# Low part of the keys kept twice, so that both products of the attention scores read 128 rows; indexer heads two at a time

## The chip, the cores and the metric

The program runs on one core of a Trainium2 chip. The metric is device time in microseconds (us), the median of three runs. The engines are named as in the profile: PE is TensorE's matrix multiply and PEld its weight loads, DVE is VectorE, ACT is ScalarE, POOL is GpSimd, and SP is SyncE, whose queue issues the DMAs.

## What is computed

A decoder trunk of four residual blocks on 1024 tokens of width 1024, in float32. Layer 0 is attention of two kinds (eight "forgetting" heads with a data-dependent bias, four differential heads with two softmax maps each), then a gated feed-forward block. Layer 1 is sparse attention of eight heads, whose keys an indexer picks, beside eight stick-breaking heads, then a second feed-forward block. The part that matters here, cut from the reference:

```
# every attention: scores of 64-wide heads, for 128 queries at a time
s = jnp.einsum('bqhd,bkhd->bhqk', qb, k).astype(jnp.float32) * scale
...
# the indexer of the sparse heads: four heads of 64, one key for all of them
logits = jnp.einsum('bqhd,bkd->bqhk', iqb, ik).astype(jnp.float32)
score = jnp.einsum('bqhk,bqh->bqk', jax.nn.relu(logits), iwb.astype(jnp.float32))
score = jnp.where(kpos[None, None, :] <= qpos[None, :, None], score, -jnp.inf)
_, sel = lax.top_k(score, top_k)          # top_k = 256
```

## The kernel before

Each float32 operand of a product is held as a rounded high part and a low part, the rest. A general product is three matmuls (`three`): high by high, high by low, low by high. The scores do it with two. A query block of a head stands as a stack of 128 rows, 64 of the high part and 64 of the low part (`evac_q`; of the two heads of a pair one has the high part on top, the other the low part). The high part of the keys, `kh`, is kept twice, in both halves of the rows (`evac_k`: ACT copies the PSUM result to one tile, and three DMAs between tiles of SBUF move halves so that each of two tiles has its head's rows twice). So one matmul of 128 rows gives high by high and low by high at once. The low part of the keys, `kl`, has the rows of both heads in one tile, each once. The second matmul takes the 64 rows of the query's high part and the 64 rows of this head's low keys:

```python
self.mm(s[:, c:c + w], q, KH[c // 512][:, :w], True, False)
self.mm(s[:, c:c + w], q[r], KL[c // 512][r, :w], False, last)
```

Keys come in chunks of at most 512 columns (c). Query block i (128 queries, i from 0 to 7) has 128 (i + 1) keys, so blocks 0 to 3 have one chunk and blocks 4 to 7 two: 12 chunks a head, and as many pairs of a `kh` and a `kl` matmul. A third, bfloat16 matmul adds the causal mask at the last block where there is one (`cmask`, `smask`). The scores lie in `psS`, which has two buffers of 1024 columns.

Layer 0 makes 16 such sets of scores (eight heads, and four with two maps each), layer 1 eight stick-breaking heads (`stick`) and eight sparse ones (`dsa`). With the indexer's 40 pairs (four heads, query blocks 2 to 7) there are 32 x 12 + 40 = 424 pairs.

The engines' order is static. `heads` runs the heads one after the other: for each, the rows of scores and softmax of query blocks 0 to 7 (`sm`) are woven with the transposes and value products of the head before (`av`), and with pieces of a generator (`fill`) that projects the queries, keys and values of later heads. A scheduler with a model of the engines' times then sets the order on each engine; an engine takes its instructions in that order. The SP queue too is taken in order: an instruction on it that waits holds back all that stand behind it.

In layer 1 the indexer (`index`) comes first: per half of the tokens four projections (`proj_tok`), transposes, `evac_q` of both pairs of heads into four tiles `iq`, then for each query block the four heads' scores, a Relu on ACT to `rl` and an accumulation on DVE to `sc`. The 256 best of each row are found by bisection on the bits of the scores (`topk`, 32 rounds): for three of six query blocks DVE counts what is over the bound (L988, written to scratch `jv`), for the others ACT does (L990, scratch `junk`). A round is issued behind a scan of the stick-breaking heads (L754), and the sparse heads need the result.

Of the kernel before, what the change touches and what calls it, by code (L numbers as in the profile page):

```python
# [13 lines left out]
I32 = mybir.dt.int32  # L14
U32 = mybir.dt.uint32
# [26 lines left out]
class Halves:  # L42
    """what is made of each half of the tokens, made when first asked for"""
# [10 lines left out]
class Net:  # L54
# [13 lines left out]
    # ---------------------------------------------------------------- tools  # L68
# [22 lines left out]
    def new_x(self):  # L91
        """eight token tiles of x"""
        X = [self.vp.tile([P, 4, D], F32, name="x", tag="v", bufs=2) for _ in range(2)]
        return [X[t // 4][:, t % 4] for t in range(NT)]

    def new_v(self):
        """values of four heads of 64 (or two of 128)"""
        return self.vp.tile([P, NT, 2, 2, P], F32R, name="v", tag="v", bufs=2)

    def identity(self):  # L100
# [3 lines left out]
        self.junk = cst.tile([P, D], mybir.dt.int8, name="junk")  # L104
# [97 lines left out]
    def mean_square(self, src, n):  # L202
        """1/sqrt(mean(src^2) + eps), a column"""
# [8 lines left out]
    def norm_half(self, xt, g):  # L212
        """four token tiles, normed and transposed and split: hT hi and lo"""
# [17 lines left out]
    def three(self, out, sh, sl, mh, ml, start, stop):  # L231
        """out += s.T @ m with both operands split; s stationary"""
# [4 lines left out]
    def proj_T(self, w, h):  # L237
        """[128 columns, 512 tokens]; a generator that returns them"""
# [7 lines left out]
    def proj_tok(self, units, h, t, n):  # L246
        """[128 tokens, n columns]; units: (hi, lo) pieces over d"""
# [10 lines left out]
    # ------------------------------------------------------- q, k, v stacks  # L258
# [24 lines left out]
    def scores(self, i, Q, KH, KL, r, mask):  # L283
        """psum scores of query block i; the operands are pairs of halves"""
# [3 lines left out]
        for c in range(0, n, 512):  # L288
# [3 lines left out]
            self.mm(s[:, c:c + w], q[r], KL[c // 512][r, :w], False, last)  # L292
# [4 lines left out]
    def pair(self, qs, ks):  # L297
        """two heads' operands of the scores"""
        (QA, QB), (KA, KB, KL) = zip(*qs), zip(*ks)
        return (QA, KA, KL, slice(0, 64)), (QB, KB, KL, slice(64, 128))  # L300

    def projected(self, us, h, gate):
        """a pair of heads; a generator"""
# [13 lines left out]
    def av(self, pt, H, half):  # L317
        """transposes the P blocks of a half of the queries, and sums over keys; a generator"""
# [51 lines left out]
    def chain(self, jobs):  # L370
        """jobs: (gate, load, body): the weights of a job are loaded before the body of the one before"""
# [28 lines left out]
    def after(self, n, f):  # L400
        """f is traced n pieces from now"""
        self.later.append([n, f])
# [8 lines left out]
    def weave(self, A, B, nb, rate):  # L411
        """the pieces of A and the generator B (of nb pieces) in step, with rate pieces of fill"""
# [40 lines left out]
    def evac_head(self, pool, feat):  # L453
        """stores the products of v hi and of v lo, [64, 512] each, of the head's output"""
# [10 lines left out]
    def softmax_rows(self, pool, i, s, bias, tag=""):  # L465
        """p = exp(s + bias - max); returns p and its sum"""
# [3 lines left out]
        m = pool.tile([P, 1], F32, name="mx", tag="mx", bufs=6)  # L470
        l = pool.tile([P, 1], F32, name="sm", tag="sm", bufs=6)
# [9 lines left out]
    def rope(self, v, M, t, pool):  # L481
        """v: [128 tokens, M, >=16]; the first 16 of each are turned, in place"""
# [3 lines left out]
        tm = pool.tile([P, 4, M, 8], F32, name="rp", tag=f"rp{M}", bufs=2)  # L486
# [8 lines left out]
    def v_split(self, ps, V, t, n):  # L495
        """psum [128 tokens, heads x n] to hi n | lo n of each head"""
# [5 lines left out]
    # ------------------------------------------------------------- layer 0  # L502
    def even_attn(self, h):
        nc, tc, A = self.nc, self.tc, self.A
        with ExitStack() as st:
# [62 lines left out]
            def fox(hd):  # L568
# [5 lines left out]
                def sm(i):  # L574
# [5 lines left out]
                    r = pp.tile([P, 1], F32, name="rc", tag="rc", bufs=6)  # L580
# [39 lines left out]
            def diff(hd):  # L620
# [3 lines left out]
                def sm(i):  # L624
# [3 lines left out]
                    m2 = pp.tile([P, 1], F32, name="mx", tag="mx", bufs=6)  # L628
                    l2 = pp.tile([P, 1], F32, name="sm", tag="sm", bufs=6)
# [5 lines left out]
                    r1 = pp.tile([P, 1], F32, name="rc", tag="rc", bufs=6)  # L635
                    r2 = pp.tile([P, 1], F32, name="rd", tag="rd", bufs=6)
# [44 lines left out]
            def zipped(f, g):  # L681
                """the pieces of f, and with each a piece of g"""
# [29 lines left out]
    # ------------------------------------------------------------- layer 1  # L712
    def odd_attn(self, h):
        nc, tc, A = self.nc, self.tc, self.A
        unit = partial(self.wunit, lo_eng="vector")
        with ExitStack() as st:
# [53 lines left out]
            def dsa_q(g, us):  # L770
                """rotated queries of four heads, to memory"""
# [10 lines left out]
            def dsa_load():  # L782
                """what the sparse attention needs, into the room of h"""
# [54 lines left out]
            def dsa(hd):  # L838
# [6 lines left out]
                def sm(i):  # L845
# [6 lines left out]
                    r = pp.tile([P, 1], F32, name="rc", tag="rc", bufs=6)  # L852
# [47 lines left out]
    def index(self, h, ix, iw, sc, chd, cld, krd):  # L900
        """latent keys, rope key (both to memory), and the scores of the indexer; a generator"""
        nc, A = self.nc, self.A
        IK = [self.qk.tile([P, 512], F32R, name="kh", tag="kh", bufs=6) for _ in range(2)]
        IL = [self.qk.tile([P, 512], F32R, name="kl", tag="kl", bufs=4) for _ in range(2)]
# [36 lines left out]
        for half in range(2):  # L941
            IQ = [ix.tile([P, 512], F32R, name=f"iq{a}", tag=f"iq{a}", bufs=1) for a in range(4)]
# [8 lines left out]
            for a in range(2):  # L951
                self.evac_q(tr(xs, a * P, (a + 1) * P), IQ[2 * a], IQ[2 * a + 1])
            yield
            for i in range(max(2, 4 * half), 4 * half + 4):
# [3 lines left out]
                for a in range(4):  # L958
                    r = slice(0, 64) if a % 2 == 0 else slice(64, 128)
                    s = self.scores(i, (IQ[a],) * 2, IK, IL, r, None)  # L960
                    rl = self.Y("rl")
                    nc.scalar.activation(rl[:, :n], s, AF.Relu)
                    nc.vector.scalar_tensor_tensor(sc[i], rl[:, :n], iw[:, i, a:a + 1], sc[i],
                                                   op0=ALU.mult, op1=ALU.add)
                    yield
# [418 lines left out]
```

## Time and profile before

| | |
|---|---|
| median of three runs | 2906.18 us |
| lowest and highest run | 2903.67 and 2909.28 us |
| span of the profiled execution, first to last instruction | 2899.5 us |
| time of the profiled execution itself | not listed apart from its span; the median of the runs is 6.7 us above the span |
| PE busy | 2776.9 us, 96% of the span |
| DVE, ACT, POOL busy | 1780.4, 1324.4, 790.2 us |
| mean granted TensorE clock | 0.975 of full speed |

Read it so: the span is what the trace covers, and the 6.7 us between it and the median is taken as what lies around it. Matmuls are pipelined and the ends of their records are modelled, so the busy time of PE holds overlaps and stalls; what one matmul costs is seen from its start to the start of the next. Attention of layer 0 takes some 60 to 590 us, its feed-forward block is done by some 1430 us, the indexer's scores lie between 1500 and 1580 us, stick-breaking and the bisection between 1585 and 1930 us, the sparse heads go to 2100 us, and the rest is the second feed-forward block.

### The profile page before, as it was taken

What the parts mean: (1) busy time and instruction counts of PE and PEld (TensorE: products, weight loads), DVE (VectorE), ACT (ScalarE), POOL (GpSimd) and SP (SyncE); (2) the same over time, 40 slices, a digit from 0 to 9 for tenths busy, and PEclk for the clock granted to TensorE, in tenths of its full rate; (3) what the DMA queues carried; (4) which work ended last, traced back from release to release, by engine and by line L of the source; (5) the groups of instructions that cost most, each with busy time, mean ns of one, the idle gap of its engine ahead of it and who ended that gap; (6) DMA issues with size and microseconds to landing.
All of it is one profiled execution on the core that took longest, in us unless ns stands there. A gap on an engine that the chain in (4) does not pass through costs nothing.

```text
span 2899.5 us, 38031 instructions
## 1 busy us (share of the span) xinstructions
PE 2776.9 (96%) x14352; PEld 2237.3 (77%) x14352; DVE 1780.4 (61%) x2561; ACT 1324.4 (46%) x2218; POOL 790.2 (27%) x1039
## 2 busy tenths in 40 slices
PE   7999999989899999999999999889998999999998
PEld 6778788779688888787887777546697888887886
DVE  3554554544777777443434998987646777776344
ACT  4444543432444444333334777646624444443232
POOL 0333433440433333000130333343504333330000
PEclk9999999989999999999999999779999999999999
DMA  5331221332232223441211222313531322223421
GB/s 113 107 88 42 74 50 38 102 116 88 69 98 75 78 87 120 142 152 44 88 52 48 66 72 87 87 39 73 172 109 66 101 82 73 87 84 139 166 77 58
DMA packets 118952, 254.47 MB, mean 88 GB/s; under 512 B 36136, under 2 KB 39336, under 8 KB 118640
## 3 DMA queue, kind: packets, MB, share of 16 engines
q1 hardware_dynamic: 118768, 252.04, 28.2%
q8 instruction: 113, 1.85, 0.3%
q14 instruction: 71, 0.58, 0.1%
HBM read 168.33 MB, written 56.92 MB: 78 GB/s over the span
## 4 chain that ended last, share of the span: by engine, by line
PE 84%; DVE 8%; ACT 2%; issue 2%; DMA 2%; POOL 1%; SPq 1%; POOLq 0%; DVEq 0%; ACTq 0%
PE psB L82 38%; PE psS L82 31%; PE psO L82 11%; PE psB L345 3%; DVE t L754 2%; DVE jv L988 1%; DVE ptl L188 1%; PE psB L1127 1%; DMA ro<-ot 0%; SPq L131 0%; PE psB L225 0%; PE psB L897 0%; DVE xn L1116 0%; DVE T_vector L1002 0%; DVE la L188 0%
## 5 line engine op out<-in xcount | busy, mean ns | idle before, releaser
L188 DVE TENSOR_TENSOR ptl<-psB,pth 128x512 fp32r<-128x512 f32 x280 | 182.2, 658 | 108.3 <-ACT pth L351 99.7
L82 PE MATMUL psB<-ha,hh 128*128 128x256 f32 (+1 forms) x768 | 222.8, 291 | 6.2 <-DVE kl L188 3.1
L82 PE MATMUL psB<-la,hh 128*128 128x256 f32 (+1 forms) x768 | 218.5, 285 | 0.0
L82 PE MATMUL psB<-ha,hl 128*128 128x256 f32 (+1 forms) x768 | 218.1, 285 | 0.0
L351 ACT ACTIVATE pth<-psB 128x512 fp32r<-128x512 f32 x280 | 158.4, 574 | 126.8 <-PE psB L345 86.7
L188 DVE TENSOR_TENSOR al<-ar,ah 128x512 fp32r<-128x512 f32 x88 | 61.0, 693 | 251.0 <-ACT ah L1228 248.2
L209 POOL TENSOR_TENSOR rs<-rs,mhalf 128x1 f32<-128x1 f32 x48 | 33.1, 693 | 627.6 <-DVE rs L208 627.3
L188 DVE TENSOR_TENSOR la<-ra,ha 128x1024 fp32r<-128x1024 f32 (+1 forms) x92 | 116.9, 1271 | 139.8 <-ACT ha L1134 112.0
L1228 ACT ACTIVATE ah<-ar 128x512 fp32r<-128x512 f32 x88 | 55.5, 631 | 311.2 <-PE psO L82 298.1
L345 PE MATMUL psB<-identf,p 128*128 128x128 f32 x1008 | 172.9, 283 | 13.5 <-DVE p L640 6.6
L82 PE MATMUL psS<-kh,qs 128*128 128x512 f32 (+2 forms) x384 | 166.9, 435 | 18.6 <-ACT p L474 5.6
L82 PE MATMUL psS<-kl,qs 64*128 64x512 f32 (+2 forms) x384 | 178.9, 466 | 0.0
L82 PE MATMUL psO<-pth,v 128*128 128x512 f32 (+2 forms) x384 | 151.5, 402 | 6.6 <-ACT pth L351 4.1
L82 PEld LDWEIGHTS psB<-ha,hh 128*128 128x128 f32 x768 | 147.2, 192 | 9.7 <-DVE kl L188 3.6
L345 PEld LDWEIGHTS psB<-identf,p 128*128 128x128 f32 x1008 | 127.5, 145 | 34.5 <-DVE p L640 7.2
L82 PEld LDWEIGHTS psB<-la,hh 128*128 128x128 f32 x768 | 146.8, 191 | 1.3 <-issue 0.4
L1134 ACT ACTIVATE ha<-ra 128x1024 fp32r<-128x1024 f32 x44 | 46.6, 1060 | 220.3 <-DMA ra<-in_wi_dram 182.1
L82 PEld LDWEIGHTS psB<-ha,hl 128*128 128x128 f32 x768 | 146.4, 191 | 0.8 <-issue 0.6
L1134 ACT ACTIVATE hs<-sr 128x1024 fp32r<-128x1024 f32 x88 | 92.8, 1055 | 115.4 <-PE psB L82 99.7
L1169 POOL TENSOR_TENSOR sr<-rb 128x512 f32<-128x512 f32 x44 | 59.1, 1343 | 314.8 <-issue 289.6
L82 PE MATMUL psO<-ptl,v 128*128 128x512 f32 x336 | 134.1, 405 | 11.2 <-DVE ptl L188 11.0
L82 PE MATMUL psS<-la,ah 128*128 128x512 f32 x352 | 138.4, 393 | 0.4 <-DVE la L188 0.4
(360 smaller groups left out, 8365.3 us busy)
## 6 DMA issues: line engine op xcount, KB each, us to landing
ra<-in_wi_dram SPq DMA_DIRECT2D x44, 512.0 KB, 4.1
rb<-in_wi_dram SPq DMA_DIRECT2D x44, 512.0 KB, 3.6
act<-yc SPq DMA_DIRECT2D x44, 512.0 KB, 3.3
ar<-act SPq DMA_DIRECT2D x88, 256.0 KB, 2.8
wd<-in_wd_dram SPq DMA_DIRECT2D x28, 512.0 KB, 4.5
kh<-kh SPq DMA_DIRECT2D x96, 128.0 KB, 2.3
ot<-oa SPq DMA_DIRECT2D x96, 128.0 KB, 2.4
ro<-ot SPq DMA_DIRECT2D x24, 512.0 KB, 3.6
```

The costliest lines, as they stand in the source:

```text
L82: self.nc.tensor.matmul(out, lhsT, rhs, start=start, stop=stop, skip_group_check=True)
L188: getattr(self.nc, eng).tensor_tensor(dst, src, hi.bitcast(F32), op=ALU.subtract)
L209: nc.gpsimd.tensor_tensor(rs, rs, self.mhalf[:, 0:1], op=ALU.pow)
L345: nc.tensor.transpose(t[:, c:c + P], H.pr[q][:, j * P:(j + 1) * P], self.identf)
L351: nc.scalar.activation(hi[:, :used], t[:, :used], AF.Copy)
L754: scan = nc.vector.tensor_tensor_scan(t1[:, :n][:, ::-1], s[:, ::-1], self.zeros[:, 0:1].to_broadcast([P, n]), 1.0, ALU.mult, ALU.add)
L988: nc.vector.tensor_scalar(j[:, :n], x, t, 0.0, op0=op, op1=ALU.add, accum_out=out)
L1127: nc.tensor.transpose(t_[:, t * P:(t + 1) * P], xs[t][:, d * P:(d + 1) * P], self.identf)
L1134: self.nc.scalar.activation(hi, raw, AF.Copy)
L1169: nc.gpsimd.tensor_tensor(s12[:, 0:4], rv[:, 0:4], rv[:, 4:8], op=ALU.add)
L1228: nc.scalar.activation(ah, ar, AF.Copy)
```

## The change

`evac_k` now makes two tiles of low keys as it does of high ones, each with its head's 64 rows twice: `new_k` takes two `kl` tiles a head pair and half (six buffers in place of four), and three DMAs `kl<-kl` of 64 x 512 join the three `kh<-kh` (32 calls, 96 DMAs more). `scores` multiplies the whole stack of the query with the doubled low keys, so the product of the two low parts, left out before, is added. The indexer's `IL` already had its rows twice. In `index` the zeroing of `sc` moves ahead, and the heads go two at a time: two tiles `iq` in place of four, each with one buffer, so the second pair's `evac_q` can write only after the last score of the first pair. Scratch: `jv` and `te` are int8 in place of bfloat16, `rp` has one buffer in place of two, `mx`, `sm`, `rc`, `rd` four in place of six. The remaining lines of the diff are comments.

```diff
     def new_k(self):
-        return [self.qk.tile([P, 512], F32R, name=n, tag=n, bufs=b) for n, b in (("kh", 6), ("kh", 6), ("kl", 4))]
+        return [self.qk.tile([P, 512], F32R, name=n, tag=n, bufs=b) for n, b in (("kh", 6), ("kh", 6), ("kl", 6), ("kl", 6))]
...
-    def evac_k(self, ps, KA, KB, KL):
+    def evac_k(self, ps, KA, KB, LA, LB):
         self.nc.scalar.activation(KA, ps, AF.Copy)
-        self.lo("vector", KL, ps, KA)
-        for dst, src in ((KB[64:128], KA[64:128]), (KB[0:64], KA[64:128]), (KA[64:128], KA[0:64])):
-            self.nc.sync.dma_start(dst.bitcast(F32), src.bitcast(F32))
-        return KA, KB, KL
+        self.lo("vector", LA, ps, KA)
+        for A, B in ((KA, KB), (LA, LB)):
+            for dst, src in ((B[64:128], A[64:128]), (B[0:64], A[64:128]), (A[64:128], A[0:64])):
+                self.nc.sync.dma_start(dst.bitcast(F32), src.bitcast(F32))
+        return KA, KB, LA, LB
...
-            self.mm(s[:, c:c + w], q[r], KL[c // 512][r, :w], False, last)
+            self.mm(s[:, c:c + w], q, KL[c // 512][:, :w], False, last)
...
-        tm = pool.tile([P, 4, M, 8], F32, name="rp", tag=f"rp{M}", bufs=2)
+        tm = pool.tile([P, 4, M, 8], F32, name="rp", tag=f"rp{M}", bufs=1)
...
-            for a in range(2):
-                self.evac_q(tr(xs, a * P, (a + 1) * P), IQ[2 * a], IQ[2 * a + 1])
-            yield
             for i in range(max(2, 4 * half), 4 * half + 4):
                 n = P * (i + 1)
                 nc.gpsimd.memset(sc[i][:, :n - P], 0.0)
                 nc.gpsimd.tensor_scalar(sc[i][:, n - P:], self.cmask, 1.0, 1.0, op0=ALU.mult, op1=ALU.mult)
-                for a in range(4):
-                    r = slice(0, 64) if a % 2 == 0 else slice(64, 128)
-                    s = self.scores(i, (IQ[a],) * 2, IK, IL, r, None)
...
+            for b in range(2):
+                IQ = [ix.tile([P, 512], F32R, name=f"iq{a}", tag=f"iq{a}", bufs=1) for a in range(2)]
+                self.evac_q(tr(xs, b * P, (b + 1) * P), *IQ)
+                yield
+                for i in range(max(2, 4 * half), 4 * half + 4):
+                    n = P * (i + 1)
+                    for a in range(2):
+                        s = self.scores(i, (IQ[a],) * 2, IK, IL, None)
...
-                j = jpool.tile([P, S], BF16, name="jv", tag="jv", bufs=1)
+                j = jpool.tile([P, S], I8, name="jv", tag="jv", bufs=1)
...
```

Where instructions move. On the SP queue, at the first pair of heads of layer 0 (`ra` are weights, `qs` and `ql` the query stacks, `nb` and `ndr` the bias rows), the rows stand so before:

```order
L272 DMA qs<-qs 64x512
L272 DMA qs<-ql 64x512 x2
L280 DMA kh<-kh 64x512 x3
L272 DMA qs<-qs 64x512
L195 DMA ra<-in_w0t_dram 128x1024
L272 DMA qs<-ql 64x512 x2
L533 DMA ndr<-nrow 8x1024
```

and so in the changed kernel:

```order
L273 DMA qs<-qs 64x512
L273 DMA qs<-ql 64x512 x2
L282 DMA kh<-kh 64x512 x2
L282 DMA kl<-kl 64x512 x2
L282 DMA kh<-kh 64x512
L282 DMA kl<-kl 64x512
L273 DMA qs<-qs 64x512
L196 DMA ra<-in_w0t_dram 128x1024
L273 DMA qs<-ql 64x512 x2
L536 DMA ndr<-nrow 8x1024
```

Three copies of low keys stand between the copies of high keys and all that follows, here the next query stack, a piece of weights and the bias rows.

On PE, at a query block 4 of layer 0 whose second chunk of keys is newly made (`identf,p` are transposes for the value product), the order before is:

```order
L82 MATMUL psS<-kh,qs 128x512
L82 MATMUL psS<-kl,qs 128x512
L82 MATMUL psS<-kh,qs 128x256
L82 MATMUL psS<-kl,qs 128x256
L82 LDWEIGHTS identb
L82 MATMUL psS<-cmask,identb 128x128
L345 MATMUL psB<-identf,p_2121 128x128 x3
L82 MATMUL psS<-kh,qs 128x512
```

and in the changed kernel:

```order
L83 MATMUL psS<-kh,qs 128x512
L83 MATMUL psS<-kl,qs 128x512
L83 MATMUL psS<-kh,qs 128x256
L348 MATMUL psB<-identf,p_2145 128x128 x3
L83 MATMUL psS<-kh,qs 128x512
L83 MATMUL psS<-kl,qs 128x512
L83 MATMUL psS<-kh,qs 128x256
L83 MATMUL psS<-kl,qs 128x256
L83 LDWEIGHTS identb
L83 MATMUL psS<-cmask,identb 128x128
L83 MATMUL psS<-kl,qs 128x256
L83 LDWEIGHTS identb
```

The second product with the new low keys has moved behind the transposes and behind the scores of the next block. The same happens at a handful of other places; elsewhere the order of PE in the attention is as before.

On PE in the indexer, second half of the tokens, in the changed kernel (`iq_13668` and `iq_13669` are the first pair of heads, `iq_13799` the first of the second pair):

```order
L83 MATMUL psS<-kh,iq_13668 128x512
L83 MATMUL psS<-kl,iq_13668 128x512
L83 MATMUL psS<-kh,iq_13669 128x512
L83 MATMUL psS<-kl,iq_13669 128x512
L83 MATMUL psB<-ha,hh 128x256
L83 MATMUL psB<-la,hh 128x256
L83 MATMUL psB<-ha,hl 128x256
...
L83 MATMUL psS<-kh,iq_13799 128x512
L83 MATMUL psS<-kl,iq_13799 128x512
L83 MATMUL psS<-kh,iq_13799 128x256
L83 MATMUL psS<-kl,iq_13799 128x256
```

Between the last score of the first pair and the first of the second stand 48 matmuls of 256 columns from `fill`. Before, the four heads of a block followed each other with some 20 such matmuls after every two, and there was no such boundary within a half.

## Rows read from the trace of the kernel before

**Rows 1.** The page, part 1: busy time, share of the span, instructions.

```profile
PE 2776.9 (96%) x14352; PEld 2237.3 (77%) x14352; DVE 1780.4 (61%) x2561; ACT 1324.4 (46%) x2218; POOL 790.2 (27%) x1039
```

**Rows 2.** Windows: busy us (x instructions) of PE PEld DVE ACT POOL, clock, DMA share.

```profile
62.00:590.00 528.00, 521.99 (x3117) 414.67 (x3115) 269.84 (x581) 243.00 (x512) 198.07 (x383) 0.99 0.26 73
...
1500.00:1605.00 105.00, 102.44 (x525) 75.20 (x524) 49.92 (x68) 45.83 (x76) 16.13 (x36) 0.99 0.19 51
1605.00:1870.00 265.00, 245.54 (x1278) 189.07 (x1277) 252.21 (x528) 200.44 (x409) 88.93 (x150) 0.93 0.28 77
1870.00:1960.00 90.00, 74.01 (x290) 46.29 (x289) 75.73 (x133) 43.69 (x87) 39.04 (x29) 0.80 0.21 49
1960.00:2100.00 140.00, 135.18 (x698) 94.48 (x698) 93.83 (x222) 93.90 (x201) 63.75 (x61) 1.00 0.43 121
```

**Rows 3.** Timeline of PE: start, duration, instruction (psS rows are scores).

```profile
464.37 0.28 PE L82 MATMUL psB<-ha,hl 128*128 128x256 f32 x1
464.49 0.39 PE L82 MATMUL psS<-kh,qs 128*128 128x512 f32 x1
464.81 0.49 PE L82 MATMUL psS<-kl,qs 64*128 64x512 f32 x1
465.23 0.38 PE L82 MATMUL psS<-kh,qs 128*128 128x256 f32 x1
465.55 0.38 PE L82 MATMUL psS<-kl,qs 64*128 64x256 f32 x1
465.86 0.23 PE L82 MATMUL psS<-cmask,identb 128*128 128x128 bf16 x1
465.90 0.48 PE L82 MATMUL psS<-kh,qs 128*128 128x512 f32 x1
466.31 0.49 PE L82 MATMUL psS<-kl,qs 64*128 64x512 f32 x1
466.73 0.39 PE L82 MATMUL psS<-kh,qs 128*128 128x256 f32 x1
467.05 0.38 PE L82 MATMUL psS<-kl,qs 64*128 64x256 f32 x1
467.36 0.23 PE L82 MATMUL psS<-cmask,identb 128*128 128x128 bf16 x1
```

**Rows 4.** The same windows for instructions on kl alone: PE PEld DVE.

```profile
62.00:590.00 528.00, 85.01 (x188) 34.76 (x188) 10.94 (x16) 0.99 0.26 73
...
1500.00:1605.00 105.00, 23.83 (x52) 9.50 (x52) 1.36 (x2) 0.99 0.19 51
1605.00:1870.00 265.00, 35.61 (x74) 14.54 (x74) 4.09 (x6) 0.93 0.28 77
1870.00:1960.00 90.00, 18.82 (x35) 7.62 (x35) 2.74 (x4) 0.80 0.21 49
1960.00:2100.00 140.00, 31.86 (x72) 12.98 (x71) 2.77 (x4) 1.00 0.43 121
```

**Rows 5.** The SP queue's waits: total us, times, longest.

```profile
SPq L280 <- DMA kh<-kh: 39.0, 27, 1.8
```

**Rows 6.** PE's waits: total us, times, longest.

```profile
PE psS L82 <- DMA qs<-ql: 0.9, 1, 0.9
```

**Rows 7.** Tile kh: ns min/median/max, first and last start; DMA to landing.

```profile
L280 SPq DMA_DIRECT2D kh<-kh x96: 461/476/1514, 70.5 to 2038.5; - x96
...
DMA to landing us min/median/max: 2.2/2.3/10.4
```

**Rows 8.** Tile iq, the same columns.

```profile
L82 PEld LDWEIGHTS psS<-kh,iq x40: 186/186/192, 1500.3 to 1579.7; 128*128 128x128 f32 x40
...
L82 PEld LDWEIGHTS psS<-kl,iq x40: 182/183/183, 1500.7 to 1580.1; 64*128 64x128 f32 x40
...
L269 ACT ACTIVATE iq<-psB x4: 591/594/603, 1494.0 to 1524.7; 128x512 fp32r<-128x512 f32 x4
```

**Rows 9.** Source line L988, the same columns: counts of the bisection on DVE.

```profile
L988 DVE TENSOR_SCALAR_CACHE_REDUCE jv<-sc,C_vector x99: 718/1003/1151, 1592.4 to 1884.8; 128x512 bf16<-128x512 f32 x33, 128x768 bf16<-128x768 f32 x33, 128x896 bf16<-128x896 f32 x33
```

More of the change, by code (lines that the diff above doesn't have):

```diff
@@ L14 @@
 I32 = mybir.dt.int32
+I8 = mybir.dt.int8
 U32 = mybir.dt.uint32
@@ L103, in identity @@
         nc.gpsimd.memset(self.mhalf, -0.5)
-        self.junk = cst.tile([P, D], mybir.dt.int8, name="junk")
+        self.junk = cst.tile([P, D], I8, name="junk")
         self.g_attn = cst.tile([P, 2, KT], F32, name="g_attn")
@@ L273, in evac_q, with scores @@
         return QA, QB
-    def evac_k(self, ps, KA, KB, KL):
+    def evac_k(self, ps, KA, KB, LA, LB):
         self.nc.scalar.activation(KA, ps, AF.Copy)
-        self.lo("vector", KL, ps, KA)
-        for dst, src in ((KB[64:128], KA[64:128]), (KB[0:64], KA[64:128]), (KA[64:128], KA[0:64])):
-            self.nc.sync.dma_start(dst.bitcast(F32), src.bitcast(F32))
-        return KA, KB, KL
-    def scores(self, i, Q, KH, KL, r, mask):
+        self.lo("vector", LA, ps, KA)
[3 more added lines that the diff above has]
+        return KA, KB, LA, LB
+    def scores(self, i, Q, KH, KL, mask):
         n = P * (i + 1)
@@ L469, in softmax_rows @@
         pv = p
-        m = pool.tile([P, 1], F32, name="mx", tag="mx", bufs=6)
-        l = pool.tile([P, 1], F32, name="sm", tag="sm", bufs=6)
+        m = pool.tile([P, 1], F32, name="mx", tag="mx", bufs=4)
+        l = pool.tile([P, 1], F32, name="sm", tag="sm", bufs=4)
         if bias is None:
@@ L579, in sm @@
                     p, l = self.softmax_rows(pp, i, s, (p, p))
-                    r = pp.tile([P, 1], F32, name="rc", tag="rc", bufs=6)
+                    r = pp.tile([P, 1], F32, name="rc", tag="rc", bufs=4)
                     nc.vector.reciprocal(r, l)
@@ L627, in sm @@
                     n = P * (i + 1)
-                    m2 = pp.tile([P, 1], F32, name="mx", tag="mx", bufs=6)
-                    l2 = pp.tile([P, 1], F32, name="sm", tag="sm", bufs=6)
+                    m2 = pp.tile([P, 1], F32, name="mx", tag="mx", bufs=4)
+                    l2 = pp.tile([P, 1], F32, name="sm", tag="sm", bufs=4)
                     s = self.scores(i, *s2, self.cmask)
@@ L634, in sm @@
                     nc.scalar.activation(ev, s, AF.Exp, bias=m2, scale=1.0, accum_out=l2)
-                    r1 = pp.tile([P, 1], F32, name="rc", tag="rc", bufs=6)
-                    r2 = pp.tile([P, 1], F32, name="rd", tag="rd", bufs=6)
+                    r1 = pp.tile([P, 1], F32, name="rc", tag="rc", bufs=4)
+                    r2 = pp.tile([P, 1], F32, name="rd", tag="rd", bufs=4)
                     nc.vector.reciprocal(r1, l1)
@@ L851, in sm @@
                         p, l = self.softmax_rows(pp, i, s, (p, sc[i]))
-                    r = pp.tile([P, 1], F32, name="rc", tag="rc", bufs=6)
+                    r = pp.tile([P, 1], F32, name="rc", tag="rc", bufs=4)
                     nc.vector.reciprocal(r, l)
@@ L903, in index @@
         IK = [self.qk.tile([P, 512], F32R, name="kh", tag="kh", bufs=6) for _ in range(2)]
-        IL = [self.qk.tile([P, 512], F32R, name="kl", tag="kl", bufs=4) for _ in range(2)]
+        IL = [self.qk.tile([P, 512], F32R, name="kl", tag="kl", bufs=6) for _ in range(2)]
         tr = self.transposed
@@ L941, in index @@
         for half in range(2):
-            IQ = [ix.tile([P, 512], F32R, name=f"iq{a}", tag=f"iq{a}", bufs=1) for a in range(4)]
             xs = []
@@ L957, in index @@
                 nc.gpsimd.tensor_scalar(sc[i][:, n - P:], self.cmask, 1.0, 1.0, op0=ALU.mult, op1=ALU.mult)
-                for a in range(4):
-                    r = slice(0, 64) if a % 2 == 0 else slice(64, 128)
-                    s = self.scores(i, (IQ[a],) * 2, IK, IL, r, None)
[L961 to L965, printed above, removed]
+            for b in range(2):
[6 more added lines that the diff above has]
+                        s = self.scores(i, (IQ[a],) * 2, IK, IL, None)
+                        rl = self.Y("rl")
+                        nc.scalar.activation(rl[:, :n], s, AF.Relu)
+                        nc.vector.scalar_tensor_tensor(sc[i], rl[:, :n], iw[:, i, 2 * b + a:2 * b + a + 1], sc[i],
+                                                       op0=ALU.mult, op1=ALU.add)
+                        yield
     def topk(self, pool, jpool, sc):
@@ L1024, in topk @@
                 nc.vector.tensor_scalar(cnt[:, j:j + 1], cnt[:, j:j + 1], -1.0, float(TOPK), op0=ALU.mult, op1=ALU.add)
-                e = jpool.tile([P, S], BF16, name="te", tag="jv", bufs=1)[:, :n]
+                e = jpool.tile([P, S], I8, name="te", tag="jv", bufs=1)[:, :n]
                 nc.vector.tensor_scalar(e, sc[i], v, 1.0, op0=ALU.is_equal, op1=ALU.mult)
```

4 lines of the change are left out of this document (2 added, 2 removed).

## Prediction

> **What bounds the kernel now.** First the page's busy line [rows 1]: PE is busy for 96% of the span and no other engine for more than 61%. Since those ends are modelled, I then read the stretches that hold the 424 pairs of score matmuls in the windows [rows 2]. In layer 0's attention PE is busy 521.99 of 528 us, DVE 269.84: PE binds, with much room elsewhere. In the indexer (1500 to 1605) PE has 102.44 of 105. From 1605 to 1870, where the bisection runs beside the stick-breaking heads, DVE has 252.21 of 265: here DVE binds, and PE's time is worth little. From 1870 to 1960 DVE has 75.73 of 90 and the granted clock is 0.80, the mean of stretches at 2.4 and at 1.2 GHz: nobody is full, and work alternates. In the sparse heads (1960 to 2100) PE has 135.18 of 140, DVE and ACT 94: PE again.
>
> Then one place of PE row by row [rows 3], by starts, not durations. The projection matmul at 464.37 and its successor at 464.49 are 0.12 us apart for 256 columns, so 512 columns flow in 0.24. The scores that follow don't: `kh` of 512 columns takes 0.32 to the next start, `kl` 0.42, `kh` of 256 columns 0.32, `kl` 0.31. The four hold 1536 columns, 0.72 us at the pace of the projection, and take 1.37 (464.49 to 465.86). The next block, which starts behind a mask, takes 1.46 (465.90 to 467.36). The excess is 0.65 and 0.74 us for two pairs, 0.33 to 0.37 a pair. It sits on both sides of the 64-row product, `64*128` in the row, and the mask behind it starts late too but itself lets the next matmul start 0.04 us later. So the stall belongs to going into and out of 64 rows, not to scores as such.
>
> **The change part by part.**
>
> *All 128 rows.* With `kl` doubled, both products are of the form that the projections have. I take their pace for them: 0.35 us less a pair, between the two blocks read. The pairs by stretch are the counts of `kl` on PE [rows 4]: 188, 52, 74, 35, 72; three or so fall outside and are left out. At full worth that is 421 x 0.35 = 147 us. What part is seen in the span depends on the stretch:
> - layer 0: 188 x 0.35 = 66. DVE would go from 51% to 58% of a stretch of 462 us, so PE still binds. I take off 8 for the late low keys (below): 58.
> - indexer: 52 x 0.35 = 18, less 4 for its new boundary (below): 14.
> - 1605 to 1870: 74 x 0.35 = 26, but DVE idles for 265 - 252.21 = 12.8 us alone, which caps it. Some of that idle time is DVE waiting for scores, not all: 9.
> - 1870 to 1960: 35 x 0.35 = 12; DVE's idle time is 14.3, and part of the alternation is DVE's own chain: 7.
> - sparse heads: 72 x 0.35 = 25, DVE and ACT at 67% have room; 4 off for softmax rows that now wait for each other: 21.
>
> Sum 58 + 14 + 9 + 7 + 21 = 109 us.
>
> What the trace of before can't show is a float32 product of 128 rows directly before a bfloat16 mask, since `kl` always stands between. Lower bound nothing (the mask is followed by a float32 weight load and that costs no stall, 465.86 to 465.90 [rows 3]); upper bound the whole exit stall of 0.19 us that `kl` before a mask has now (0.31 against 0.12 at 465.55). With 208 masks (144 in layer 0 and at the first blocks of the sparse heads, 64 in the stick-breaking heads) that is 40 us, 27 of it where PE binds. I take nothing, since the passing from mask to `kh` is the nearer row. The Trainium skill, "TensorEngine Tiling (Array Packing)", section Tiling Modes, says that changing the tiling mode drains TensorE; by that rule the type of the operands doesn't matter and the mask costs nothing, which no run here has shown yet.
>
> *Three more DMAs per `evac_k`.* Each is an issue of 0.476 us on SP and lands in 2.3 us; 96 of them add 46 us to a queue with much idle time [rows 7]. The third copy waits for the first two, whose tile it overwrites; now SP stands in these waits 39.0 us, 27 times, at most 1.8 [rows 5]. In the new order the low keys' third copy is last, so the operands of a chunk are complete up to 3 x 0.476 + 1.8 = 3.2 us later than now. Queued behind are query stacks and weights, which are asked for a job ahead. In the whole span PE waited for such a copy once, 0.9 us [rows 6], so operands are mostly early. The exception is a chunk that is used as soon as it is made, where the order puts the last product behind the next block's. I price 16 such places in layer 0 (one a set of scores, second half of the tokens) at 0.5 us: 8, from both ends 0 and 16 x 3.2 = 51.
>
> *The indexer's order.* The second pair of a half may be written only after the first pair's last score: ACT 0.594 [rows 8], then a copy, issued and landed like that of a key in 0.476 and 2.3 [rows 7], then a second one behind it: 0.59 + 2 x (0.48 + 2.3) = 6.2 us. The same chain now takes 1494.0 to 1500.3 = 6.3 us [rows 8]. Covered by 48 matmuls at 0.12 = 5.8 us in the second half, more in the first; a wait of about 0.5 us remains. Four scores in a row without filler before it fill the two `psS` buffers and wait for ACT and DVE; I allow 3.5 us. Together 4; bounds 0, and 2 x 6.2 = 12 with no cover.
>
> *Scratch.* `jv` in int8: the counts take 718 to 1151 ns for 512 to 896 elements [rows 9], 1.28 to 1.4 ns an element, so they are not packed now and nothing is lost by a narrower output; I take nothing. Lower end nothing too; upper end, with 105 such counts of 1.0 us, 5% would be 5 us in the stretch that DVE binds. `rp` is written and read by POOL alone, in its order. `mx`, `sm`, `rc`, `rd` with four: `psS` has two buffers, so DVE is at most two or three rows ahead of ACT; POOL, which frees `rc`, is busy 198 of 528 us [rows 2]. Nothing, and if that cover were gone, a DVE wait in a stretch where DVE has room. The ring of `kl` becomes that of `kh`, which is held just as long: nothing.
>
> The profiled span becomes 2899.5 - 109 = 2790; the median stood 6.7 above its span, so **2797 us**.
>
> **Rivals.**
>
> *Half of it is given back.* PE at a faster pace meets the latency from score to softmax to transpose; the stretches of DVE give nothing; a mask costs its 0.19. Then layer 0 gives 35, the indexer 8, the sparse heads 12: 55, so about 2850. For it: the SP waits above and DVE's 95%. Against it: 6 us of PE idle time in layer 0 with DVE at half load. Chance 0.20.
>
> *All of it.* Nothing is late, and the stretches of DVE give their whole idle time: 66 + 18 + 12.8 + 12 + 25 = 134, so 2772, or some us less if the 1.2 GHz pieces shrink as well. Chance 0.12.
>
> *The rows don't matter.* The stall could be of the alternation of two operands or of the query stack being loaded twice, not of 64 rows; then it stays. With 8 for late keys and 4 for the indexer the time would be 2918. Against it: projections alternate three operands and flow [rows 3]. Chance 0.03. The Trainium skill, "TensorE: Matmul & The Clock Gate", section "Why this matters for your kernels", says that a matmul of few rows takes the same time as one of 128, the gain being only in running several at once; that rule sees no gain here. On weight loads the trace agrees: 183 ns for 64 rows, 186 for 128 [rows 8].
>
> *The low keys come late everywhere.* This is the case on the slow side: 32 calls of `evac_k`, each holding PE. It would have to be over 109 / 32 = 3.4 us a call, more than the whole 3.2 us found above, so it decides only where SP also holds back the weights behind it; at 4 us, 128, the time is 2925. Chance 0.02.
>
> **How the numbers follow.** The likeliest case has 0.61 (2775 to 2824: the sum a fifth larger, or a quarter smaller), half given back 0.20, all of it 0.12, the two without gain 0.05, a mix that ends near the old time 0.02. The range reaches into the first two rivals: 2768 to 2842. A measurement of this kernel tells 0.2%, some 6 us, from no change. Faster 0.93, same 0.02, slower 0.05.
>
> **What would show it.** `kl` on PE as `128*128`, and from one `kh` to the next `kl` 0.24 us for 512 columns; a pair some 0.35 us shorter everywhere, in DVE's stretch too. Layer 0's attention over 55 to 60 us sooner, the sparse heads some 20 us shorter, the stretch of the bisection nearly as long as now with DVE over 97%. `jv` rows as long as before. PE's waits with a few us for `kl<-kl` and about 1 for `iq<-ql`. I'd be wrong if `kl` to mask still takes 0.31 for 256 columns, if PE waits for `kl<-kl` more than 20 us in total, or if idle time on PE in layer 0 grows by more than 20 us.

## The result, and the profile after

The changed kernel takes **2824.16 us** (median of 4, 2820.68 to 2829.55) beside 2907.34 for the kernel before on the same chip: a ratio of 0.9716 with a 95% interval of 0.97 to 0.9732, 83 us less. The forecast was 109 us less, 2797, with a range of 2768 to 2842. The profiled span is 2818.9 us (before 2899.5), the mean granted clock 0.975 in both.

Page, part 1, of the changed kernel (the form of [rows 1]):

```profile
PE 2648.2 (94%) x14352; PEld 2227.4 (79%) x14352; DVE 1775.2 (63%) x2561; ACT 1322.4 (47%) x2220; POOL 790.0 (28%) x1039
```

PE executes as many matmuls as before and is busy 129 us less. Where that happens is seen in PE's timeline of two score blocks with a mask, to be laid beside [rows 3]:

```profile
417.94 0.39 PE L83 MATMUL psS<-kh,qs 128*128 128x512 f32 x1
418.17 0.40 PE L83 MATMUL psS<-kl,qs 128*128 128x512 f32 x1
418.40 0.28 PE L83 MATMUL psS<-kh,qs 128*128 128x256 f32 x1
418.52 0.28 PE L83 MATMUL psS<-kl,qs 128*128 128x256 f32 x1
418.65 0.23 PE L83 MATMUL psS<-cmask,identb 128*128 128x128 bf16 x1
418.69 0.47 PE L83 MATMUL psS<-kh,qs 128*128 128x512 f32 x1
419.00 0.39 PE L83 MATMUL psS<-kl,qs 128*128 128x512 f32 x1
```

The four products now take 0.71 us (417.94 to 418.65) where they took 1.37: 512 columns in 0.23, 256 in 0.12, the pace of the projections. The step that no row of before could price, a float32 product of 128 rows directly before the bfloat16 mask, is the one from 418.52 to 418.65: 0.13 us, no stall. One delay is left, `kh` behind a mask (418.69 to 419.00, 0.31 where 0.23 is the pace).

The windows, set to the same places of the program as in [rows 2] (layer 0 from 62, the indexer from 1455, bisection and stick-breaking heads from 1524, their end from 1809, sparse heads from 1848):

```profile
62.00:544.00 482.00, 466.28 (x3140) 409.24 (x3139) 268.56 (x585) 245.33 (x517) 200.39 (x384) 1.00 0.35 93
1455.00:1524.00 69.00, 64.87 (x398) 57.65 (x397) 30.42 (x39) 27.69 (x47) 8.77 (x30) 1.00 0.33 83
1524.00:1809.00 285.00, 243.10 (x1396) 202.81 (x1395) 267.73 (x556) 215.12 (x436) 95.14 (x156) 0.93 0.30 82
1809.00:1848.00 39.00, 26.59 (x118) 18.39 (x117) 35.38 (x56) 18.24 (x30) 14.60 (x11) 0.81 0.48 107
1848.00:1997.00 149.00, 131.29 (x741) 104.86 (x740) 121.03 (x281) 106.18 (x235) 77.87 (x74) 0.93 0.40 104
```

PE still binds in layer 0, but its idle time there is 482 - 466.28 = 15.7 us, against 6.0 [rows 2]. In the bisection's stretch DVE is at 94%, no fuller than before (95%).

Since those windows are cut by hand, the lengths below go by the starts of the first and last score matmuls of each kind; a table of the kernels that matter (us; e1, e3 and e4 are experiments of the next section):

| stretch | before | e4, pairs alone | e1, 64 rows | e3, grouped | changed |
|---|---|---|---|---|---|
| layer 0, first score to last | 513.7 | 508.7 | 509.6 | 490.7 | 463.5 |
| indexer, first score to last | 79.7 | 82.8 | 82.7 | 73.6 | 69.4 |
| from there to the last stick-breaking score | 318.6 | 323.3 | 328.0 | 315.1 | 313.4 |
| from there to the last sparse score | 180.5 | 180.9 | 180.4 | 171.1 | 159.4 |
| all the rest of the span | 1807.0 | 1805.7 | 1816.8 | 1810.8 | 1813.2 |

The change gives 50, 10, 5 and 21 us in the four stretches, and loses 6 in the rest. PE's waits (us in total, times, longest) have new leaders, among them the low keys:

```profile
PE psS L83 <- DVE t L757: 13.5, 13, 3.6
...
PE psB L83 <- DVE kl L189: 8.5, 3, 4.8
...
PE psS L83 <- DMA kl<-kl: 4.0, 4, 1.7
PE psS L83 <- DMA qs<-ql: 2.6, 1, 2.6
```

The first two lie in the stretch behind the indexer, the second but for 0.6 us. Of the first, the stick-breaking heads' scan `t`, the kernel before has:

```profile
PE psS L82 <- DVE t L754: 2.8, 6, 0.7
```

SP's waits, where [rows 5] had one row, and the tile of the low keys, the same columns as [rows 7]:

```profile
SPq L282 <- DMA kl<-kl: 38.0, 28, 4.2
SPq L282 <- DMA kh<-kh: 21.8, 29, 6.3
```

```profile
L282 SPq DMA_DIRECT2D kl<-kl x96: 461/541/967, 71.5 to 1962.6; - x96
DMA to landing us min/median/max: 2.2/2.4/7.7
```

A low key's copy is issued in 0.54 us, lands in 2.4, and SP stands 21 us longer than before in these waits. Of that 4.0 us reach PE. Tile `iq`, to be laid beside [rows 8]: the 40 `kl` weights now load in 188 ns with 128 rows (183 with 64), and the first score to the last is 69 us:

```profile
L83 PEld LDWEIGHTS psS<-kh,iq x40: 186/188/192, 1454.5 to 1523.5; 128*128 128x128 f32 x40
...
L83 PEld LDWEIGHTS psS<-kl,iq x40: 187/188/192, 1454.6 to 1523.8; 128*128 128x128 f32 x40
```

The counts with the int8 scratch take 723 to 1148 ns, where [rows 9] has 718 to 1151:

```profile
L992 DVE TENSOR_SCALAR_CACHE_REDUCE jv<-sc,C_vector x99: 723/1004/1148, 1535.6 to 1824.3; 128x512 int8<-128x512 f32 x33, 128x768 int8<-128x768 f32 x33, 128x896 int8<-128x896 f32 x33
```

### The profile page after: what moved, and what is told of

It is laid out like the page before. It is cut to its first block, busy times and chain, and to the rows that moved or that the text cites. A ratio compares the mean times of both kernels' runs of the same rounds, so it can differ in the third digit from the quotient of the medians.

```text
span 2818.9 us, 38226 instructions
## 1 busy us (share of the span) xinstructions
PE 2648.2 (94%) x14352; PEld 2227.4 (79%) x14352; DVE 1775.2 (63%) x2561; ACT 1322.4 (47%) x2220; POOL 790.0 (28%) x1039
## 4 chain that ended last, share of the span: by engine, by line
PE 76%; DVE 10%; DMA 4%; ACT 4%; issue 3%; POOL 3%; SPq 1%; POOLq 0%; DVEq 0%; ACTq 0%
PE psB L83 36%; PE psS L83 26%; PE psO L83 10%; PE psB L348 2%; DVE t L757 2%; DVE jv L992 2%; DVE ptl L189 1%; DMA ro<-ot 1%; PE psB L1131 1%; DMA kl<-kl 1%; POOL ol L189 1%; ACT junk L994 0%; POOL ro L1060 0%; DMA ot<-oa 0%; ACT pth L354 0%
## 5 line engine op out<-in xcount | busy, mean ns | idle before, releaser
L83 PE MATMUL psB<-ha,hh 128*128 128x256 f32 (+1 forms) x768 | 223.7, 292 | 13.5 <-DVE kl L189 8.5
L83 PE MATMUL psS<-kh,qs 128*128 128x512 f32 (+2 forms) x384 | 153.9, 401 | 43.2 <-DVE t L757 13.5
L759 POOL TENSOR_TENSOR p<-p,t 128x127 f32<-128x127 f32 (+3 forms) x64 | 78.4, 1226 | 225.0 <-DVE t L757 154.1
L83 PE MATMUL psS<-kl,qs 128*128 128x512 f32 (+2 forms) x384 | 135.5, 359 | 4.0 <-DMA kl<-kl 4.0
```

The lines of the kernel that those rows point to most:

```text
L83: self.nc.tensor.matmul(out, lhsT, rhs, start=start, stop=stop, skip_group_check=True)
L759: nc.gpsimd.tensor_tensor(p[:, :n - 1], p[:, :n - 1], t1[:, 1:n], op=ALU.mult)
```

## Experiments

My theory: the gain is the passage of PE between 128 and 64 rows, seen whole where PE binds. Against it: the stall belongs to something else that the change moved; the copies of the low keys or the order by pairs eat the missing 26 us; or DVE's load holds the bisection's stretch. Every ratio is to the kernel before on the same chip.

**e1: the changed kernel with 64 rows.** Copies, order and scratch stay.

```diff
-            self.mm(s[:, c:c + w], q, KL[c // 512][:, :w], False, last)
+            self.mm(s[:, c:c + w], q[r], KL[c // 512][r, :w], False, last)
```

> The changed kernel, but the second product of the scores takes 64 rows again; the copies of the low keys, the indexer's order and the scratch stay changed. It leaves out the product of the two low parts, as the kernel before does. If the stall belongs to going into and out of 64 rows, the whole gain is lost: 2905 to 2925 us, kl 0.42 us from start to start at 512 columns. If the gain came from the order or the scratch, it stays near 2824.

Measured 2917.3 us, ratio 1.0055 (1.004 to 1.0071). The whole gain is gone and 16 us more (12 to 21 by the interval). The stall is back, as PE's timeline of e1 shows (512 columns of `kl` take 0.42 us to the next start):

```profile
464.54 0.39 PE L83 MATMUL psS<-kh,qs 128*128 128x512 f32 x1
464.87 0.49 PE L83 MATMUL psS<-kl,qs 64*128 64x512 f32 x1
465.29 0.38 PE L83 MATMUL psS<-kh,qs 128*128 128x256 f32 x1
465.60 0.38 PE L83 MATMUL psS<-kl,qs 64*128 64x256 f32 x1
465.92 0.23 PE L83 MATMUL psS<-cmask,identb 128*128 128x128 bf16 x1
```

So the 128 rows alone are worth 1.0055 - 0.9716 = 3.4%, 98 us. In the table they give, from e1 to the changed kernel, 46, 13, 15 and 21 us. (The order on PE is set anew for every kernel: at 663 of 14352 places e1 has another matmul than the changed kernel, so a small part of these numbers may be order.) What isn't the rows costs 16 us, but in the profiled executions 10 of them lie in "all the rest of the span", which holds no scores: between layer 0's last score and the indexer's first, the granted clock is at 1.2 GHz for 44.4 us in e1 and for 27.3 before, by the clock records of the two traces.

**e2: the changed kernel without the copies of the low keys.** Both heads read one tile, and the second is not made.

```diff
-        for A, B in ((KA, KB), (LA, LB)):
+        for A, B in ((KA, KB),):
...
-        return KA, KB, LA, LB
+        return KA, KB, LA, LA
```

> The changed kernel without the three copies of low keys: both heads of a pair multiply all 128 rows of one tile, whose other 64 rows are the other head's, so the product of the low parts is another number. If late low keys cost what I priced, 8 us, it runs at 2816 (2808 to 2824). If they hold back the queue, under 2800. If the copies are hidden, 2824 within 6.

Measured 2815.81 us, ratio 0.9707 (0.9694 to 0.9721): 3 us under the changed kernel, within the intervals. Layer 0's scores take 458.7 us instead of 463.5, and the other stretches move by less than 2. A part of the 5 us is the clock, since the changed kernel's execution has 3.4 us at 1.2 GHz there and this one none. So the 96 copies cost at most 5 us, in layer 0, and the ratio doesn't tell that from nothing.

**e3: the kernel before, its products grouped by rows.** The second loop over the chunks is the only edit: both high products of a block, then both low ones, so that 144 blocks of two chunks pass once into 64 rows instead of twice.

```diff
             self.mm(s[:, c:c + w], q, KH[c // 512][:, :w], True, False)
+        for c in range(0, n, 512):
+            w = max(min(512, n - c), 256)
+            last = mask is None or c + 512 < n
             self.mm(s[:, c:c + w], q[r], KL[c // 512][r, :w], False, last)
```

> The kernel before, but where a query block has two chunks of keys, both 128-row products go first and then both 64-row products: the same matmuls with two passages between 64 and 128 rows in place of four, in 144 scores. If the passage costs, 144 x 0.30 to 0.35 = 43 to 50 us on PE, some 70% of it seen: 2870 to 2880. If a 64-row product is slow by itself, no change: 2907 within 6.

Measured 2861.03 us, ratio 0.9869 (0.9854 to 0.9883): 38 us less with every 64-row product still there, a little more than the 27 to 37 expected. PE's timeline of this kernel (x2 joins two matmuls in one row):

```profile
448.71 0.51 PE L82 MATMUL psS<-kh,qs 128*128 128x512 f32 x2
449.16 0.61 PE L82 MATMUL psS<-kl,qs 64*128 64x512 f32 x2
449.70 0.23 PE L82 MATMUL psS<-cmask,identb 128*128 128x128 bf16 x1
449.74 0.59 PE L82 MATMUL psS<-kh,qs 128*128 128x512 f32 x2
450.26 0.61 PE L82 MATMUL psS<-kl,qs 64*128 64x512 f32 x2
450.81 0.23 PE L82 MATMUL psS<-cmask,identb 128*128 128x128 bf16 x1
```

A block of 512 and 256 columns, twice over, takes 0.99 and 1.07 us, where the columns alone need 0.72: 0.27 and 0.35 of stall with one passage in and out, against 0.65 and 0.74 with two [rows 3]. The edit removes 144 of 424 passages, a third, and wins 38 of the 98 us that e1 puts on all of them. The stall is counted by passages, not by 64-row products. In the first block 0.10 us of it come before the first 64-row product (448.71 to 449.16, for 0.35 of columns) and 0.19 from there to the mask.

**e4: the kernel before with the indexer's heads in pairs**, that part of the diff alone.

> The kernel before with the indexer's heads two at a time and nothing else. By my sum the new boundary costs 4 us: 2911 (2907 to 2919). If the order is a gain of its own, 2900 or less.

Measured 2912.14 us, ratio 1.0033 (1.0021 to 1.0046): the order costs some 10 us (6 to 13), not 4. In its profiled execution, the quickest of its five, 3 of them are in the indexer (79.7 to 82.8) and 5 in the stretch behind it (318.6 to 323.3). Layer 0, by contrast, is 5 us shorter there, 508.7 against 513.7, although PE's instructions up to the indexer's own stand in the same order in both. The windows tell why; the kernel before, then e4:

```profile
450.00:500.00 50.00, 50.00 (x293) 39.99 (x292) 23.27 (x43) 19.42 (x44) 19.48 (x53) 0.86 0.16 43
```

```profile
450.00:500.00 50.00, 50.00 (x334) 40.83 (x333) 26.50 (x50) 22.69 (x50) 24.22 (x62) 1.00 0.17 44
```

PE is busy for all 50 us in both, but executes 293 matmuls at a mean granted clock of 0.86 and 334 at 1.00. So 5 of the 50 us of layer 0 are a piece at 1.2 GHz in the one profiled execution of before, and no work of the change.

**e5: a shorter chain of copies.** Each head's 64 key rows go from ACT and DVE straight to its own tile, one copy each behind them.

```diff
-        self.nc.scalar.activation(KA, ps, AF.Copy)
-        self.lo("vector", LA, ps, KA)
-        for A, B in ((KA, KB), (LA, LB)):
-            for dst, src in ((B[64:128], A[64:128]), (B[0:64], A[64:128]), (A[64:128], A[0:64])):
-                self.nc.sync.dma_start(dst.bitcast(F32), src.bitcast(F32))
+        for H, L, r, f in ((KA, LA, slice(0, 64), slice(64, 128)), (KB, LB, slice(64, 128), slice(0, 64))):
+            self.nc.scalar.activation(H[r], ps[r], AF.Copy)
+            self.lo("vector", L[r], ps[r], H[r])
+            for A in (H, L):
+                self.nc.sync.dma_start(A[f].bitcast(F32), A[r].bitcast(F32))
```

> The changed kernel, but each head's 64 key rows go from PSUM to their own tile directly, so every copy is one hop (four in place of six, none behind another); ACT and DVE take two half operations for one whole, 32 x 0.6 and 32 x 0.68 us more. If late keys still hold PE, 2815 or less. If the copies are hidden, the added work shows where DVE binds, 6 x 0.68 = 4 us: 2824 to 2830.

Measured 2830.36 us, ratio 0.9761 (0.9742 to 0.978): slower than the changed kernel by 0.45%, 13 us, more than either reading allowed. The first score comes 5.5 us sooner (75.5), the last of layer 0 7.6 us later (552.1). Its row of the evacuation on ACT (ns min/median/max):

```profile
L279 ACT ACTIVATE kh<-psB x64: 567/592/596, 70.2 to 1963.4; 64x512 fp32r<-64x512 f32 x64
```

A half tile of 64 rows takes 592 ns, a whole one of 128 takes 597 in the changed kernel, so ACT pays twice for the same keys, and DVE likewise (688 and 684 ns). The shorter chain doesn't earn it back: the copies were nearly hidden already, as e2 says.

**e6: one count moved from DVE to ACT** in the bisection of the changed kernel.

```diff
-            groups = [("vector", [3, 5, 6]), ("scalar", [2, 4, 7])]
+            groups = [("vector", [3, 6]), ("scalar", [2, 4, 5, 7])]
```

> The changed kernel with the bisection's 768-column block counted on ACT in place of DVE: 33 x 1.09 = 36 us less on DVE, 37 more on ACT. If DVE binds that stretch, so that PE's gain was lost there, it gets 12 to 22 us shorter: 2802 to 2812. If something else holds it, 2824 within 6, or slower where ACT becomes the bound.

Measured 2833.92 us, ratio 0.9773 (0.9754 to 0.9793): slower. The stretch behind the indexer grows from 313.4 to 327.0 us. DVE now waits there for ACT's counts (`junk`); e6, then the changed kernel:

```profile
DVE Y_scalar L1005 <- ACT junk L994: 22.3, 10, 4.3
```

```profile
DVE Y_scalar L1005 <- ACT junk L994: 3.5, 2, 3.1
```

**e8: three shared buffers for the indexer's query stacks** in place of two with one each.

```diff
-                IQ = [ix.tile([P, 512], F32R, name=f"iq{a}", tag=f"iq{a}", bufs=1) for a in range(2)]
+                IQ = [ix.tile([P, 512], F32R, name="iq", tag="iq", bufs=3) for a in range(2)]
```

> The changed kernel with three buffers shared by the indexer's query tiles in place of one for each of two, so the second pair's first tile needn't wait. If the boundary between the pairs costs the 3 us seen in the indexer's stretch and what follows, 2815 to 2821; if the loss is in the order, 2824 within 4.

Measured 2820.09 us, ratio 0.9732 (0.9708 to 0.9755), no change that can be measured; the time lies in both ranges of the expectation, so the ratio decides. The indexer takes 68.1 us (69.4). The tile that the second pair waits for is not what the order by pairs costs.

**e7: the edits of e5, e6 and e8 together.**

> The last three edits together: one-hop copies, the 768-column block counted on ACT, three buffers for the indexer's query tiles. If their effects add, 2795 to 2808; if one undoes another, 2808 or more.

Measured 2857.15 us, ratio 0.9854 (0.9836 to 0.9873): worse than each; 478.7 us in layer 0, 339.0 behind the indexer. The three edits alone lost 0.45, 0.57 and 0.16%, together 1.4%.

**e12: the changed kernel again**, beside the next three.

> The changed kernel itself, beside the next three on one chip: a ratio of 0.970 to 0.973 to the kernel before, as first measured. It is what the three are compared with.

Measured 2820.36 us, ratio 0.9716 (0.9698 to 0.9734). The stretches repeat: 463.7, 68.6, 313.8 and 156.3 us.

**e9: fewer elements for DVE.** The counts of the block of 896 keys read 128 of its columns, and the number to be reached is made smaller in proportion.

```diff
-                    count(eng, sc[i], C.bitcast(F32)[:, j:j + 1], cnt[:, j:j + 1], ALU.is_ge)
+                    x = sc[i][:, :P] if i == 6 else sc[i]
+                    count(eng, x, C.bitcast(F32)[:, j:j + 1], cnt[:, j:j + 1], ALU.is_ge)
```

> The changed kernel, DVE's counts for the 896-column block over 128 columns alone (it leaves out the rest of that count, so another set of keys is chosen): some 33 x 0.8 = 26 us less on DVE, nothing more on ACT. If DVE's load holds the stretch of the bisection, 12 to 25 us faster than the changed kernel. If the rounds' chain over ACT holds it, or PE, within 5 us of it.

Measured 2816.66 us, ratio 0.9705 (0.9684 to 0.9727), not to be told from e12. In the windows of the stretch behind the indexer, e12 and then e9:

```profile
1522.60:1836.40 313.80, 263.56 (x1492) 216.18 (x1491) 293.89 (x593) 230.91 (x463) 106.34 (x164) 0.94 0.31 83
```

```profile
1521.30:1824.90 303.60, 261.16 (x1479) 216.28 (x1478) 269.58 (x589) 228.42 (x459) 105.65 (x164) 0.92 0.32 85
```

DVE has 24 us less to do and the stretch is 10 shorter: DVE falls to 89%, PE stands at 86%. The total hardly moves, since the sparse heads then take 160.0 us (156.3) and the feed-forward block behind them 827.6 (822.7), with 29.7 us at 1.2 GHz (17.9). PE's order also differs from e12's at 647 places, and e10's at 644, so small differences here are not load alone.

**e10: the same for ACT**, the block of 1024 keys.

> The changed kernel, ACT's counts for the 1024-column block over 128 columns alone (it leaves out the rest of that count): some 32 x 0.8 = 26 us less on ACT, nothing changed on DVE. If DVE's load holds the stretch, within 5 us of the changed kernel. If DVE and ACT wait for each other in turn, 5 to 15 us faster.

Measured 2821.52 us, ratio 0.9717 (0.9699 to 0.9735), the stretch 313.0 us: nothing.

**e11: both.**

> Both of these cuts in the counts together. If DVE alone holds the stretch, as the cut on DVE alone; if both engines do in turn, the sum of the two, 20 to 35 us faster than the changed kernel; if PE, no change.

Measured 2814.24 us, ratio 0.9697 (0.9677 to 0.9716), the stretch 306.7 us. With less on both engines the interval still overlaps that of e12.

## Why the prediction was right, and which terms were mis-sized

**The mechanism held.** What the prediction read from the trace came out: `kl` is a product of 128 rows at the projections' pace, and the passage from a float32 product to the mask costs nothing, for which I had bounds of 0 to 40 us. The experiments agree: without the 128 rows there is no gain (e1), and with a third of the passages gone 39% of the gain is there (e3). None of the three signs of being wrong was seen: `kl` to mask takes 0.13 us, PE waits 4.0 us for `kl<-kl`, and its idle time in layer 0 grew by 10. The Trainium skill, "TensorEngine Tiling (Array Packing)", section Tiling Modes, which ties the drain to a change of mode, agrees with e3 and with the mask's 0.13 us. The rule of the Trainium skill, "TensorE: Matmul & The Clock Gate", section "Why this matters for your kernels", by which a matmul of few rows takes as long as one of 128, saw no gain; it speaks of a single matmul, and in this stream 512 columns take 0.42 us to the next start with 64 rows (e1) and 0.23 with 128.

**The rivals.** "The rows don't matter" falls with e1 and "the low keys come late everywhere" with e2. "All of it" falls by the time. The time alone doesn't decide between the forecast and "half of it is given back": 2824 lies 27 us from 2797 and 26 from 2850, on the edge of the range I gave the likeliest case (2775 to 2824), and 83 us is 76% of the forecast. The parts decide. That rival had 35, 8 and 12 us in layer 0, the indexer and the sparse heads and a cost at each mask; the runs show 45 to 50, 10, 21 and no such cost. But it was nearer than the forecast in the stretch of the bisection.

**What PE saved and what came back.** Windows set to the table's stretches give PE's busy time; what is left of a stretch is idle. From the kernel before to the changed one (us):

| stretch | forecast | PE busy less | PE idle more | shorter |
|---|---|---|---|---|
| layer 0 | 58 | 60.0 | 9.7 | 50.2 |
| indexer | 14 | 13.6 | 3.3 | 10.3 |
| bisection and stick-breaking heads | 9 + 7 | 27.9 | 22.7 | 5.2 |
| sparse heads | 21 | 30.3 | 9.2 | 21.1 |
| sum | 109 | 131.8 | 44.9 | 86.8 |

Two terms were mis-sized: the worth of the rows, 147 us before deductions, was 132 (some 126 without a piece at half the clock in the execution of before, see layer 0), and 45 came back where the forecast let 38 be lost. Split by e1, the forecast of the rows was 66 + 18 + 9 + 7 + 25 = 125 us and they gave 98. Its deductions were 8 + 4 + 4 = 16, and all that isn't the rows cost 16; that these agree is luck, since 10 of the 16 lie in the rest of the span, where there are no scores and the forecast had priced nothing (e1).

**The price of a pair, 0.35 us, became 0.30 by what is left.** Over all of layer 0 the time from each score matmul's start to the next, less its columns at the projections' pace and counting at most 0.25 us each, sums to 68.4 us in e4, whose layer 0 is that of before at full clock. That is 0.36 for each of 192 pairs, as I had read it. But I took the bare pace for the new form, and in the changed kernel 10.3 us are left: 58.1 us are gone, 0.30 a pair. Some 6 of the 10 are the first `kh` behind a mask or a transpose, which still comes 0.08 us late. The stick-breaking and the sparse heads lost some 28 us each over 96 pairs, 0.29. Over all four stretches the same sum gives 154 us for the 424 passages of the kernel before and 100 for the 280 of e3, 0.36 each in both.

**Layer 0: 58 forecast, 50 seen, 45 earned.** Beside e4, PE is busy 54 us less and idle 9 more (6.9 to 15.7). By the list of its waits in layer 0 that is 3.2 us for `kl<-kl`, 2.6 for one query stack (1.2 in e1), and waits of 1 to 2 us on ACT, DVE and POOL each; the late keys, priced at 8, were at most 5 (e2). The remaining 5 of the 50 seen were the clock of the one execution before that I had summed against.

**Indexer: 14 forecast, 10 measured.** Of the 52 `kl` matmuls behind my 18 us, 12 belong to the stick-breaking heads, which follow the last indexer score at 1580.1 in the same window. Its own 40 pairs at 0.35 are 14, and PE is busy 13.6 less; the order cost 3 here (4 forecast). But by e4's times the order costs some 10 in all, most of it outside the indexer, where I had priced nothing for it. That the second pair's query stacks arrive late is not the reason (e8); which of the moved steps it is stays open.

**Bisection and stick-breaking heads: 9 + 7 forecast, 5 measured.** Before, then changed, from the indexer's last score to the last stick-breaking one:

```profile
1580.10:1898.70 318.60, 292.45 (x1500) 220.71 (x1499) 297.10 (x596) 233.09 (x463) 108.41 (x165) 0.93 0.27 72
```

```profile
1524.00:1837.40 313.40, 264.51 (x1492) 217.55 (x1491) 294.57 (x594) 230.30 (x462) 107.19 (x164) 0.93 0.32 84
```

PE is busy 28 us less and its idle time grows from 26 to 49; of its waits DVE's `t` has 13.5 where it had 2.8. The rows alone gave 15 (e1 to changed), and by the profiled executions the order by pairs took some 5 back. My reason, that DVE's load caps the gain, held only in part. I had expected DVE over 97% and it is at 94%; taking 24 us from it shortens the stretch by 10 and the total by nothing measurable (e9), and DVE then waits more for ACT (8.8 us for the counts, 11.1 for `pth`; 3.5 and 3.6 in e12). Giving its work to ACT lengthens the stretch by 14 (e6); relieving ACT does nothing (e10). No single engine's load was shown to hold this stretch. The waits fit work that passes between PE, ACT and DVE in a fixed order; which link of it is the last was not settled.

**Sparse heads: 21 forecast, 21 measured** (24 in e12's execution), partly by luck: the forecast's window held 72 of the 96 pairs, and 9 us came back where I had allowed 4. **Scratch: nothing forecast, nothing measured** in the counts' durations.

**Outside the four stretches 6 us were lost**, priced nowhere. Between layer 0's last score and the indexer's first the changed kernel takes 910.1 us with 34.1 at 1.2 GHz, the kernel before 905.5 with 27.3, and e3, which has neither copies nor pairs, 907.9 with 34.1. Behind the sparse heads it is 822.0 with 19.6 against 820.2 with 16.8. Time at 1.2 GHz does half the work of time at 2.4, so by my estimate up to 5 of the 6 us, (6.8 + 2.8) / 2, go with the granted clock; why that was lower is not shown. The 6.7 us that I put between span and median are mostly of this kind too: every execution whose span is listed takes only 1.7 to 2.2 us longer than its span, so the profiled execution of before was a quick one.

No version tried beats the changed kernel by more than the measurement can tell.

## What to carry to other kernels

Read PE by the starts of its matmuls, not by their durations: in this kernel a stream that mixes 64-row and 128-row products paid 0.36 us for each way in and out. Doubling the short operand won most of that back (98 us of 2900); grouping the products by their rows, with no data moved, won 38. Price such a stall as the difference of the two forms, since the new one may keep some of it (0.05 us a pair here), and subtract what the engines behind it will hand back. A new order of work must be priced behind its own stretch too: the indexer's pairs cost some 10 us, of which one profiled execution shows 3 in the indexer and 5 in the stretch that followed.

## What the runs showed of the hardware that was not expected

- The passage into 64 rows is dear enough that reordering alone, with the same matmuls, gave a ratio of 0.9869.
- The same PE instructions in the same order ran at a mean granted clock of 0.86 in one execution and 1.00 in another (450 to 500 us, kernel before and e4), with PE busy throughout in both. The piece at 1.2 GHz begins at 472.8 us and lasts 13.7; PE was busy for all of the time before it from 450 on. In the profile of before I had taken layer 0's length as it stood; one profiled execution carries such pieces, 5 us here.
- The spread between executions of one kernel goes with the granted clock: of 27 timed executions of the kernel before, on three chips, those with a mean of 0.977 or more took 2893 to 2898 us, those with 0.973 or less 2901 to 2910.
- ACT takes as long for 64 rows of 512 elements as for 128 (592 and 597 ns), so splitting an evacuation by rows doubles its cost.
